# An encoder layer on one core: the down weights' differences loaded and stored through GpSimd's queue, with each store in two halves

## The chip, the cores and the metric

The kernel runs on one core of one Trainium2 chip. The metric is the device time of one execution in microseconds (us). Three executions are known of the kernel before; the median is 1974.39 us.

## The reference, cut to what matters

One encoder layer on 1024 tokens plus 16 meta tokens, width 1024, all in float32. The part that matters here is the last one, a SwiGLU block with 2816 hidden columns:

```python
h2 = rmsnorm(h_res, norm2_w[l])
gu = h2 @ w_gate_up[l]                                    # 1024 x 5632
h_res = h_res + (jax.nn.silu(gu[..., :D_FF]) * gu[..., D_FF:]) @ w_down[l]   # 2816 x 1024
out = rmsnorm(h_res, final_norm_w)
```

## The kernel before, in words

**Precision.** TensorE multiplies operands of the type float32r. Every float32 operand is split in a high part (ScalarE, L101, a CAST) and a low part (VectorE, L102, a subtraction), and a product is three matmuls for each slice of the inner dimension.

**Fewer products.** Matrix products are made in the manner of Strassen: the operands are cut in 2 x 2 blocks, sums and differences of blocks are formed first, and seven block products stand for eight. The down projection at the end of the kernel (L2025 and on) needs such differences of blocks of `w_down`. They depend on weights alone, so the kernel makes them earlier, beside another stage, and parks them in DRAM in the tensors `t_d[0..10]`, from which the end reads them back (L2048 in the profile).

**The gate and up stage.** The loop at L1966 runs over 22 pairs of column blocks (gate and up), j = 0 to 21; the first ones are opened ahead of it in an order written out by hand, which ends at L1965. From there the framework's scheduler sets the order at build time: on each engine the instructions stand in one fixed order and are executed in that order, and an instruction that waits holds all that stand behind it on its engine. A pair is seven products (L1446, twelve matmuls each) into PSUM banks: P1 and P2 (part1, L1764), then S2, S1, S3, S4 and TT (L1986 to L1996). P1, S2, S3 and TT share one bank. Between them the bank has to be read: after P1 and after S2 by ScalarE (L1769, L1987), after S3 by VectorE (`add(u3, b1, u3)`, L1991, recorded as L1412 with `b<-pd,b`). In this document that last one is called **the S3 add**. TT can't start before it has ended; only the product S4 lies between S3 and TT. ScalarE copies the bank of S1 (L1989) ahead of S4 in the same way. VectorE also makes the sums and low parts of the next pair's weights (L1420 to L1423, L102).

**The differences of the down weights.** After pair j, for j = 4 to 14, the loop calls `down_sums(j - 4, ...)` (L2001, function at L1776). One call is a **block**, k = 0 to 10. It takes the tile `r` of 128 x 2 x 1024 (named `sums` in the profile; its pool has one buffer of the tag `al1`, so block k+1 uses the same memory as block k), loads its two halves from `w_down` (L1782, L1783, 512 KB each), makes four subtractions in place on VectorE (recorded as L179 `sums<-sums`), and stores the whole tile to `t_d[k]` (L1786, 1024 KB). The loads and the store are issued by SyncE (SP). Because there is one buffer, the loads of block k+1 wait until the store of block k has landed. From the first subtraction of a block to the first of the next is called a **turn**.

SyncE's queue also holds the loads of the gate and up weights (L1759, L1760, into `raw` tiles) and the stores of the activations (L1998, L1999), in an order that the scheduler made.

Of the kernel before, what the change touches and what calls it, by code (L numbers as in the profile page):

```python
# [16 lines left out]
P = 128  # L17
# [31 lines left out]
def encoder_layer(ctx: ExitStack, tc: tile.TileContext, x, meta, norm1_w, w_in, w_ba,  # L49
                  dn_conv_w, A_log, dt_bias, dn_norm_w, sc_conv_w, w_bdn, w_bsc,  # L50
                  w_out, norm2_w, w_gu, w_down, final_w, out):
    nc = tc.nc
    x, out = x[0], out[0]
    w_out, w_down = w_out[0], w_down[0]
# [10 lines left out]
    def uid(s):  # L65
        cnt["n"] += 1
        return f"{s}_{cnt['n']}"
# [110 lines left out]
    def sub(out, a, b):  # L178
        nc.vector.tensor_tensor(out=out, in0=a, in1=b, op=ALU.subtract)  # L179
# [1570 lines left out]
    HK = NF // 2  # L1750
    t_d = [dr.tile([P, 2, D], F32, name=f"t_d{k}") for k in range(HK)]
# [24 lines left out]
    def down_sums(k, behind):  # L1776

        r = ap_.tile([P, 2, D], F32, tag="al1", name=uid("sums"))
        if k == 0:
            nc.scalar.copy(r[:, 0, 0:1], behind[:, 0:1])  # L1780
        b11, b12, b21, b22 = (r[:, i // 2, 512 * (i % 2):512 * (i % 2) + 512] for i in range(4))
        nc.sync.dma_start(r[:, 0], w_down[k * P:k * P + P, :])  # L1782
        nc.sync.dma_start(r[:, 1], w_down[(HK + k) * P:(HK + k + 1) * P, :])  # L1783
        for o_, a, b in ((b11, b12, b11), (b12, b22, b12), (b22, b22, b11), (b21, b21, b22)):
            sub(o_, a, b)
        nc.sync.dma_start(t_d[k], r)  # L1786


    def load_pair(j, spread=False):
# [176 lines left out]
    for j in range(2, NF):  # L1966
# [12 lines left out]
        if j >= HK:  # L1979
            k = j - HK  # L1980
# [19 lines left out]
        if 4 <= j <= HK + 3:  # L2000
            down_sums(j - 4, sg)  # L2001
# [147 lines left out]
```

## Time and profile before

| | us |
|---|---|
| three executions | 1973.14, 1974.39, 1974.99 |
| the profiled execution, whole | 1973.36 |
| its span, first to last instruction | 1971.6 |
| TensorE (PE) busy in the span | 1957.3 |
| VectorE (DVE) busy | 1398.0 |
| ScalarE (ACT) busy | 837.7 |
| GpSimd (POOL) busy, all of it before 970 us | 108.4 |

The gate and up stage lies from about 970 us to 1760 us of the span; the blocks of `down_sums` are worked on from 1434.6 us to 1577.3 us. A row of the profile names the line, the engine, the operation and the tiles (output, then inputs). In a timeline the first number is the start in the span and the second the duration, both in us; the brackets say how long the engine was idle ahead of it and for what. `SPq` is a transfer's issue on SyncE; PEld is TensorE's weight load.

### The profile page before, as it was taken

To read this page: it belongs to the slowest core of one execution; us is meant where nothing else is said; L and a number is where in the kernel's file an instruction comes from. 1 tells how busy PE (TensorE), PEld (TensorE's weight loads), DVE (VectorE), ACT (ScalarE), POOL (GpSimd) and SP (SyncE) were. 2 spreads that over 40 slices of the span, in tenths; PEclk is the share of its full clock that TensorE was granted. 3 is DMA by queue.
4 is the path that set the end of the run, shared out by engine and by line. 5 is a ranking of instruction groups with operands and counts; after the bars stand their busy time and mean duration, and the time that the engine had idled before them with its cause. 6 is when DMAs were issued, how large, how long until landed. Compare 5 with 4: busy or idle time off the path is not lost.

```text
span 1971.6 us, 31923 instructions
## 1 busy us (share of the span) xinstructions
PE 1957.3 (99%) x11992; PEld 1719.6 (87%) x11992; DVE 1398.0 (71%) x3017; ACT 837.7 (42%) x1968; POOL 108.4 (5%) x410
## 2 busy tenths in 40 slices
PE   9999999999999999999999999999999999999998
PEld 8999999999999999888888888888888888878887
DVE  7888688888888888845954544468676765746575
ACT  6462364646464646343444211235333333324344
POOL 2011101010101010100000000000000000000000
PEclk9999999999999999999999999999999999999999
DMA  4122121212121212223246642133366654577654
GB/s 145 61 86 81 55 87 60 77 59 77 59 84 52 87 49 87 65 81 108 85 150 242 245 153 86 65 107 112 103 234 246 245 189 153 178 274 242 193 173 168
DMA packets 124704, 251.53 MB, mean 128 GB/s; under 512 B 44988, under 2 KB 46453, under 8 KB 122117
## 3 DMA queue, kind: packets, MB, share of 16 engines
q1 hardware_dynamic: 123957, 248.44, 37.8%
q8 instruction: 94, 1.54, 0.3%
q10 hardware_dynamic: 592, 1.05, 0.1%
q14 instruction: 61, 0.50, 0.1%
HBM read 181.20 MB, written 68.25 MB: 127 GB/s over the span
## 4 chain that ended last, share of the span: by engine, by line
PE 45%; DMA 3%; DVE 2%; ACT 1%; issue 0%; SPq 0%; DVEq 0%; ACTq 0%
PE pd L1446 12%; PE pe L1446 6%; PE pm L1446 4%; PE pe L2057 1%; PE pe L2055 1%; PE pe L2056 1%; PE pd L2057 1%; PE pd L2055 1%; PE pd L2056 1%; PE pe L134 1%; PE pe L135 1%; PE pd L135 1%; PE pd L134 1%; PE pe L136 1%; PE pd L136 1%; PE pm L2056 1%
## 5 line engine op out<-in xcount | busy, mean ns | idle before, releaser
L328 PE MATMUL pm<-hTh,wh 128*128 128x320 f32 (+4 forms) x1248 | 426.9, 347 | 0.3 <-ACT hTh L1096 0.2
L328 PE MATMUL pm<-hTh,wl 128*128 128x320 f32 (+4 forms) x1248 | 426.8, 347 | 0.0
L328 PE MATMUL pm<-al,wh 128*128 128x320 f32 (+4 forms) x1248 | 423.8, 345 | 0.0
L328 PEld LDWEIGHTS pm<-hTh,wh 128*128 128x128 f32 x1248 | 233.9, 188 | 10.7 <-ACT hTh L1096 0.9
L328 PEld LDWEIGHTS pm<-al,wh 128*128 128x128 f32 x1248 | 233.8, 188 | 10.7
L328 PEld LDWEIGHTS pm<-hTh,wl 128*128 128x128 f32 x1248 | 233.9, 188 | 10.2 <-POOL wl L1111 0.3
L102 DVE TENSOR_TENSOR al<-raw,ring_h 128x1024 fp32r<-128x1024 f32 x73 | 88.6, 1222 | 65.6 <-ACT ring_h L101 64.7
L101 ACT CAST ring_h<-raw 128x1024 fp32r<-128x1024 f32 x73 | 76.6, 1053 | 109.1 <-PE pe L2057 35.0
L982 DVE TENSOR_TENSOR wl<-raw,wh 128x512 fp32r<-128x512 f32 x112 | 75.3, 687 | 34.5 <-ACT wh L985 34.2
L350 DVE SCALAR_TENSOR_TENSOR kq<-ra,wc,kq 128x520 f32<-128x520 f32 x128 | 96.5, 754 | 3.5 <-ACT kq L380 2.0
L878 ACT ACTIVATE w<-pd,small 128x128 f32<-128x128 f32 x128 | 39.8, 362 | 123.4 <-PE pd L871 122.9
L483 DVE TENSOR_TENSOR tm<-fP,fN 128x135 f32<-128x135 f32 (+23 forms) x248 | 72.2, 291 | 4.8
L487 DVE TENSOR_TENSOR fP<-fP,tm 128x135 f32<-128x135 f32 (+23 forms) x248 | 71.9, 290 | 5.0
L985 ACT CAST wh<-raw 128x512 fp32r<-128x512 f32 x112 | 66.3, 624 | 3.8 <-issue 3.6
L101 ACT CAST wh<-raw 128x1024 fp32r<-128x1024 f32 x37 | 38.8, 1047 | 47.8 <-PE pe L135 10.4
L1994 ACT ACTIVATE b<-b 128x512 f32<-128x512 f32 x20 | 12.6, 632 | 101.6 <-DVE b L1412 101.6
L843 ACT ACTIVATE jk<-NP 128x128 f32<-128x128 f32 x64 | 19.9, 311 | 81.1 <-DVE NP L839 80.1
L102 DVE TENSOR_TENSOR wl<-raw,wh 128x1024 fp32r<-128x1024 f32 x37 | 45.1, 1219 | 10.2 <-ACT wh L101 10.0
L1446 PE MATMUL pd<-b_hl,wh 128*128 128x512 f32 x168 | 51.9, 390 | 0.0
L1412 DVE TENSOR_TENSOR b<-pd,b 128x512 f32<-128x512 f32 x21 | 14.5, 689 | 52.5 <-PE pd L1446 47.5
L350 DVE SCALAR_TENSOR_TENSOR vT<-ra,wc,vT 128x520 f32<-128x520 f32 x64 | 48.3, 754 | 1.4 <-ACT vT L380 0.7
L679 POOL TENSOR_TENSOR tm<-mP,mN 1x15 f32<-1x15 f32 (+7 forms) x120 | 36.9, 307 | 210.8 <-DMA mN<-ndm 202.4
(630 smaller groups left out, 4772.1 us busy)
## 6 DMA issues: line engine op xcount, KB each, us to landing
raw<-in_w_in_dram SPq DMA_DIRECT2D x72, 512.0 KB
raw<-in_w_gate_up_dram SPq DMA_DIRECT2D x44, 512.0 KB
sums<-in_w_down_dram SPq DMA_DIRECT2D x22, 512.0 KB
t_d<-sums SPq DMA_DIRECT2D x11, 1024.0 KB
raw<-s_d SPq DMA_DIRECT2D x44, 256.0 KB
raw<-t_d SPq DMA_DIRECT2D x44, 256.0 KB
act_d<-b SPq DMA_DIRECT2D x43, 256.0 KB
raw<-act_d SPq DMA_DIRECT2D x33, 256.0 KB
```

The costliest lines, as they stand in the source:

```text
L101: nc.scalar.copy(hi, src)
L102: nc.vector.tensor_tensor(out=lo, in0=src, in1=hi.bitcast(F32), op=ALU.subtract)
L134: mm(po[:m, :n], wh[:, k, :m], xhk[:, t0:t0 + n], start=(k == 0), stop=False)
L328: mm(po[:, :n], ww[:, k], f(k)[:, t0:t0 + n], start=i == 0, stop=i == 3 * KT - 1)
L350: nc.vector.scalar_tensor_tensor(out=acc, in0=raw[:, h0 + t:h0 + t + hn], scalar=wc[:, t, col:col + 1], in1=acc, op0=ALU.mult, op1=ALU.add)
L483: nc.vector.tensor_tensor(out=tv, in0=fP[:, 0:r, j:j + 1].broadcast_to([P, r, n]), in1=fN[:, j:j + 1, j + 1:32].broadcast_to([P, r, n]), o ...
L487: nc.vector.tensor_tensor(out=fP[:, 0:r, j + 1:32], in0=fP[:, 0:r, j + 1:32], in1=tv, op=ALU.subtract)
L878: nc.scalar.activation(w[d], b2[:, 2 + d], AF.Copy, scale=ce[:, c, d:d + 1])
L982: nc.vector.tensor_tensor(out=u[1][1][:, k], in0=u[2][:, k], in1=u[1][0][:, k].bitcast(F32), op=ALU.subtract)
L985: nc.scalar.copy(u[1][0][:, k], u[2][:, k])
L1446: mm(po, x[:, k], at(y, k), start=i == 0 and not add_to, stop=i == 11, skip_group_check=add_to)
L2056: mm(bank[t], h_[:, c], l_[:, hi], start=False, stop=False)
```

## The change

The two loads and the store of `down_sums` are issued by GpSimd in place of SyncE, and the store is cut in two: the first half of the tile is stored after the second subtraction, the other after the fourth. The arithmetic is the same.

```diff
-        nc.sync.dma_start(r[:, 0], w_down[k * P:k * P + P, :])
-        nc.sync.dma_start(r[:, 1], w_down[(HK + k) * P:(HK + k + 1) * P, :])
-        for o_, a, b in ((b11, b12, b11), (b12, b22, b12), (b22, b22, b11), (b21, b21, b22)):
+        nc.gpsimd.dma_start(r[:, 0], w_down[k * P:k * P + P, :])
+        nc.gpsimd.dma_start(r[:, 1], w_down[(HK + k) * P:(HK + k + 1) * P, :])
+        for i, (o_, a, b) in enumerate(((b11, b12, b11), (b12, b22, b12), (b22, b22, b11), (b21, b21, b22))):
             sub(o_, a, b)
-        nc.sync.dma_start(t_d[k], r)
+            if i % 2:
+                nc.gpsimd.dma_start(t_d[k][:, i // 2], r[:, i // 2])
```

From L1787 on, a line of the kernel after has a number that is one higher. TensorE's order is the same in both kernels. The orders of SyncE, GpSimd, VectorE and ScalarE differ.

**SyncE and GpSimd, around block 1.** On SyncE before, the transfers of blocks 0 and 1 stand among the gate and up loads and the activation stores:

```order
L1760 DMA raw_15892<-in_w_gate_up_dram 128x1024
L1759 DMA raw_15891<-in_w_gate_up_dram 128x1024
L1786 DMA t_d_14752<-sums_15505 128x2048
L1782 DMA sums_15631<-in_w_down_dram 128x1024
L1783 DMA sums_15631<-in_w_down_dram 128x1024
L1999 DMA act_d_14735<-b_2350_14860 128x512
L1998 DMA act_d_14735<-b_2350_14860 128x512
L1786 DMA t_d_14753<-sums_15631 128x2048
```

After, they stand on GpSimd's queue alone, behind its last MEMSET; in the brackets are the semaphores for which each waits (DMASW is one of GpSimd's transfers, DVE VectorE):

```order
L1783 DMA sums_15505<-in_w_down_dram 128x1024 [waits DVE_49,PE_49]
L1782 DMA sums_15505<-in_w_down_dram 128x1024 [waits Activation_49]
L1787 DMA t_d_14752<-sums_15505 128x1024 [waits DMASW1_49,DVE_49]
L1787 DMA t_d_14752<-sums_15505 128x1024 [waits DMASW0_49,DVE_49]
L1782 DMA sums_15632<-in_w_down_dram 128x1024 [waits DMASW3_49,DMASW2_49]
L1783 DMA sums_15632<-in_w_down_dram 128x1024
```

33 transfers leave SyncE's queue and 44 come to GpSimd's. The first load of a block waits for both half stores of the block ahead (DMASW2 and DMASW3).

**VectorE in pair 6.** `pd_15647` before and `pd_15649` after are the same bank, pair 6's; `sums_15756` and `sums_15758` are block 2. Before:

```order
L102 TENSOR_TENSOR wl_15890<-raw_15891,wh_15889 128x1024
L102 TENSOR_TENSOR s_hl_15092<-raw_15766,s_hl_15092 128x1024
L179 TENSOR_TENSOR sums_15756<-sums_15756 128x512
L1412 TENSOR_TENSOR b_2350_14860<-pd_15647,b_2350_14860 128x512
L179 TENSOR_TENSOR sums_15756<-sums_15756 128x512 x3
L1412 TENSOR_TENSOR b_2350_14860<-pe_15686,b_2350_14860 128x512
```

After:

```order
L102 TENSOR_TENSOR s_hl_15092<-raw_15769,s_hl_15092 128x1024
L102 TENSOR_TENSOR wl_15894<-raw_15895,wh_15893 128x1024
L179 TENSOR_TENSOR sums_15758<-sums_15758 128x512 x3
L1412 TENSOR_TENSOR b_2350_14860<-pd_15649,b_2350_14860 128x512
L179 TENSOR_TENSOR sums_15758<-sums_15758 128x512
L1412 TENSOR_TENSOR b_2350_14860<-pe_15688,b_2350_14860 128x512
```

Ahead of the S3 add (`<-pd`) stood one subtraction of block 2, and three stand there now.

**VectorE in pair 11.** `pd_16272` before and `pd_16279` after are pair 11's bank; `sums_16659` is block 9 before, and `sums_16806` is block 10 after. Before:

```order
L102 TENSOR_TENSOR mB_14825<-raw_16403,mB_14825 128x1024
L102 TENSOR_TENSOR wl_16539<-raw_16540,wh_16538 128x1024
L179 TENSOR_TENSOR sums_16659<-sums_16659 128x512 x3
L1412 TENSOR_TENSOR b_2350_14860<-pd_16272,b_2350_14860 128x512
L179 TENSOR_TENSOR sums_16659<-sums_16659 128x512
```

After:

```order
L102 TENSOR_TENSOR wl_16548<-raw_16549,wh_16547 128x1024
L102 TENSOR_TENSOR mB_14825<-raw_16411,mB_14825 128x1024
L179 TENSOR_TENSOR sums_16806<-sums_16806 128x512 x2
L1412 TENSOR_TENSOR b_2350_14860<-pd_16279,b_2350_14860 128x512
L179 TENSOR_TENSOR sums_16806<-sums_16806 128x512 x2
```

Before, the S3 add of pair 11 stands behind three subtractions of block 9, and block 10 is not begun until pair 12; now it stands behind two subtractions of block 10, the last one.

## The prediction

> **What bounds the kernel now.** I read the page's busy row first, then the stretch in which the blocks run, then who waits there, and last the chain of waits. The page's first part:
>
> ```profile
> span 1971.6 us, 31923 instructions
> PE 1957.3 (99%) x11992; PEld 1719.6 (87%) x11992; DVE 1398.0 (71%) x3017; ACT 837.7 (42%) x1968; POOL 108.4 (5%) x410
> ```
>
> TensorE is idle for 14.3 us in all, so no change that leaves its products alone can gain more than that. The stretch from 1430 to 1580 us holds all subtractions of the blocks; the view by stretches gives the length, then each engine's busy time and count, the granted clock, the DMA share and the rate:
>
> ```profile
> 1430.00:1580.00 150.00, 149.89 (x662) 123.80 (x661) 108.39 (x150) 51.29 (x72) 0.00 (x0) 1.00 0.67 242
> ```
>
> TensorE is busy in 149.89 of 150 us, at the full granted clock (1.00), and GpSimd is empty. Of the waits in that stretch, here is the only one of TensorE, and then four of the others (total, times, longest):
>
> ```profile
> PEld pd L1446 <- DVE b L1412: 0.5, 1, 0.5
> ...
> DVE sums L179 <- DMA sums<-in_w_down_dram: 16.1, 7, 4.2
> ...
> SPq L1786 <- DVE sums L179: 27.2, 11, 3.8
> SPq L1786 <- DMA sums<-in_w_down_dram: 18.2, 7, 5.1
> SPq L1782 <- DMA t_d<-sums: 15.2, 8, 4.2
> ```
>
> VectorE stands for 16.1 us in front of subtractions whose loads haven't landed; SyncE stands in front of this function's store and loads for more. Yet TensorE lost 0.5 us. So the waits are there, and they are covered. How thin the cover is shows in the chain of waits (start, duration, what):
>
> ```profile
> 1521.63 2.73 PE pd L1446 x12
> 1532.32 4.42 DMA t_d<-sums
> 1536.76 5.10 DMA sums<-in_w_down_dram
> 1541.98 0.69 DVE sums L179
> ...
> 1551.87 5.78 DMA sums<-in_w_down_dram
> 1557.74 0.70 DVE sums L179
> 1559.08 0.69 DVE b L1412
> 1559.82 5.74 PE pd L1446 x24
> ```
>
> For 35 us the chain leaves TensorE and runs through a store, loads and subtractions to the S3 add of pair 11. The blocks' turns are already the tightest thing beside TensorE.
>
> **What is removed.** 33 issues on SyncE, and with them the 27.2 + 18.2 us in which it stands in front of L1786 and the 15.2 us in front of L1782, so the gate and up loads behind them can go earlier. I cost this at nothing: in the stretch no row of the waits has ScalarE or VectorE waiting for a `raw` load, so nobody is late for those. At best the 0.5 us of TensorE goes.
>
> **What is moved: one turn more.** The deadline is read at pair 11 in the timeline (start, duration):
>
> ```profile
> 1554.11 2.88 PE L1446 MATMUL pd<-b,s_hl 128*128 128x512 f32 x12
> 1556.83 2.88 PE L1446 MATMUL pe<-b,s_hl 128*128 128x512 f32 x12
> 1559.82 2.56 PE L1446 MATMUL pd<-b,u_hl 128*128 128x512 f32 x10
> ...
> 1434.62 0.68 DVE L179 TENSOR_TENSOR sums<-sums 128x512 f32<-128x512 f32 x1
> ...
> 1556.01 0.69 DVE L179 TENSOR_TENSOR sums<-sums 128x512 f32<-128x512 f32 x1 [2.16 <-DMA sums<-in_w_down_dram]
> 1557.74 1.42 DVE L179 TENSOR_TENSOR sums<-sums 128x512 f32<-128x512 f32 x2 [1.04 <-DMA sums<-in_w_down_dram]
> 1559.08 0.68 DVE L1412 TENSOR_TENSOR b<-pd,b 128x512 f32<-128x512 f32 x1
> ```
>
> S3 and S4 start 2.72 us apart, so TT was due at 1556.83 + 2.72 = 1559.55; it began at 1559.82, 0.27 late, behind the S3 add. Block 0's first subtraction began at 1434.62 and block 9's at 1556.01: nine turns of (1556.01 - 1434.62) / 9 = 13.49 us, and with these the kernel before is just in time. In the new order block 10, not 9, stands ahead of this add, with two subtractions. A run of two and the add took from 1557.74 to 1559.08, so to be in time block 10 has to start by 1557.74 - 0.27 = 1557.47. That is **ten turns in 122.85 us, 12.29 us each**. With turns of 13.49 it would be 134.9 - 122.85 = 12.05 us late. VectorE keeps to its order, so the S3 add waits for it, then TT, then every product behind. In pair 6, with three subtractions ahead of the S3 add in place of one, the same wait comes early, so the lateness is paid in pieces along pairs 6 to 11.
>
> **What the new transfers do to a turn.** A turn in the old kernel, with the sizes of the transfers, from the timeline and the issues:
>
> ```profile
> 1453.16 0.32 SPq L1786 DMA_DIRECT2D t_d<-sums  x1
> ...
> 1457.04 0.33 SPq L1782 DMA_DIRECT2D sums<-in_w_down_dram  x1
> 1457.42 0.42 SPq L1783 DMA_DIRECT2D sums<-in_w_down_dram  x1
> ...
> 1461.73 0.69 DVE L179 TENSOR_TENSOR sums<-sums 128x512 f32<-128x512 f32 x1 [3.31 <-DMA sums<-in_w_down_dram]
> ...
> sums<-in_w_down_dram SPq DMA_DIRECT2D x22, 512.0 KB
> t_d<-sums SPq DMA_DIRECT2D x11, 1024.0 KB
> ```
>
> The store takes 3.9 us until the first load may go, and 4.7 us later the first subtraction starts.
>
> Half a store: the first half goes while subtractions three and four run, so the second half alone, 512 KB, is left on the path. I take off what 0.524 MB cost at the rate of the busiest stretch that I looked at:
>
> ```profile
> 1458.00:1463.00 5.00, 5.00 (x24) 4.13 (x23) 1.69 (x3) 0.59 (x1) 0.00 (x0) 1.00 0.94 346
> ```
>
> At 346 GB/s that is 1.5 us less per turn. GpSimd's issues: three lie in a row on a turn's path (second half store, first load, second load, which the second subtraction needs). The trace has no transfer issued by GpSimd. The nearest rows are issues of the same transfers on SyncE (least, median, most, in ns):
>
> ```profile
> L1783 SPq DMA_DIRECT2D sums<-in_w_down_dram x11: 328/432/1093, 1365.4 to 1569.5; - x11
> L1786 SPq DMA_DIRECT2D t_d<-sums x11: 319/326/327, 1440.0 to 1577.4; - x11
> L2048 SPq DMA_DIRECT2D raw<-t_d x44: 429/432/1475, 1791.8 to 1934.8; - x44
> ```
>
> From 0.33 to 1.475 us; I take the middle, 0.90, in place of 0.33, 0.33 and 0.43: 0.57 + 0.57 + 0.47 = 1.6 us more per turn. What comes after the issue I take as on SyncE. So a turn is 13.49 - 1.5 + 1.6 = 13.6 us, and ten are 136.
>
> GpSimd has nothing else to do (0.00 busy in the stretch), so issues there delay nobody but the blocks. That a third queue is used at all costs something only outside the stretch, for which the whole profiled run has 1973.36 - 1971.6 = 1.8 us; I take nothing.
>
> **Two rules of the skill.** The Trainium skill, "DMA: Bandwidth & Descriptors", section "Issuing engines are not separate DMA queues", says that all issuers share the same 16 engines and that another issuer saves only its issue time. The trace agrees as far as it goes: an issue is 0.33 us on SyncE. The same page, "Latency and other measured facts", puts the first byte at about 0.6 us for SyncE's way and 1 us for GpSimd's. No run here shows either; with 0.4 us more on a store and on a load, the turn would be 12.8 us and the sum 5 us.
>
> **The sum.** 136 - 122.85 = 13.1 us late, less the 0.5 us that TensorE lost already: +12.6 us on the profiled execution's own 1973.36, **1986.0 us**. The median of the runs before, 1974.39, lies 1.0 above that execution.
>
> Bounds. With issues at 0.33 us the turn is 12.0, under 12.29: nothing late, 1973.36 - 0.5 = 1972.9. With issues at 1.475 (+1.15, +1.15, +1.04) and loads like the chain's slow ones (5.78 for 4.7) the turn is 13.49 - 1.5 + 3.3 + 1.1 = 16.4, so 164 - 122.85 - 0.5 = +41, 2014.
>
> **The rivals.**
>
> *In time after all, not slower.* If a turn through GpSimd takes at most 12.29 us, block 10 is ready, TensorE stays full, and the time is 1972.9. What decides is 1.2 us per turn against 13.49, and the halved store alone could give it. For it: few subtractions waited for a load (count, busy time and mean, idle time ahead of them),
>
> ```profile
> L179 DVE TENSOR_TENSOR sums<-sums 128x512 f32<-128x512 f32 x44 | 30.2, 687 | 16.5 <-DMA sums<-in_w_down_dram 16.1
> ```
>
> 7 of 44 by the row above, so part of 13.49 may be the old order's own pace. Against it: SyncE's issue of 0.33 us would have to hold for GpSimd.
>
> *Far slower: GpSimd held up by VectorE.* VectorE is busy 108.39 of 150 us. If each issue had to let the running VectorE instruction end, at most the longest here,
>
> ```profile
> L102 DVE TENSOR_TENSOR mB<-raw,mB 128x1024 fp32r<-128x1024 f32 x8 | 9.7, 1220 | 0.2
> ```
>
> then three of 1.22 us per turn make it 13.6 + 3.7 = 17.3 and the sum 173 - 123.35 = +50, 2023. Against it: nothing in the stretch shows the two engines meeting. The Trainium skill, "SBUF — State Buffer", section "SBUF: two separate sides", has this as its "DVE blocks DMA" trap, but only beside VectorE's two-port modes, which a two-input operation like these rows doesn't use; by that rule it would not come.
>
> *SyncE relieved, a real gain.* The whole cover is 0.5 us, so this can't reach 0.2%.
>
> **How the numbers follow.** Forecast (5 to 25 us slower) 0.5; in time after all 0.22; 25 to 41 us slower 0.18; held up by VectorE 0.08; a gain by something not seen 0.02. The time given is the forecast's, 1986; the range 1972.9 to 2014 takes in the bounds of the issue cost and leaves out the held-up case. About 0.2% (3.9 us) is what a measurement of this kernel can tell from no change. Slower by more: 0.5 + 0.18 + 0.08 = 0.76; within: 0.21; faster: 0.03.
>
> **What would show it.** Right: TensorE's busy time is unchanged, its idle time in pairs 6 to 11 is some 13 us, ended by the S3 add (L1412) or by ScalarE's copy (L1988) that stands behind it; VectorE's wait for `sums` grows from 16.1 us; block 10's first subtraction starts near 1570, not by 1557.5; the old queue's row falls by some 23 MB and another queue has them. The issue cost is read as the gap between GpSimd's two loads of a block. Wrong: TensorE full with the blocks done early (issue cheap), gaps of whole VectorE instructions ahead of GpSimd's issues, or idle time elsewhere, at the end above all, where `t_d` is read.

## The result, and the profile after

| | us |
|---|---|
| before, median of six | 1974.22 (1973.04 to 1976.26) |
| after, median of six | 1987.62 (1985.41 to 1992.16) |
| ratio, 95% interval | 1.0074 (1.0063 to 1.0085) |
| the profiled execution of after, whole | 1990.61 |

The kernel is 13.4 us slower by the medians; 1986.0 was forecast. The page of after, its busy row and its two large queues (packets, MB, share):

```profile
span 1988.9 us, 31974 instructions
...
PE 1963.4 (99%) x11992; PEld 1723.7 (87%) x11992; DVE 1399.6 (70%) x3017; ACT 837.9 (42%) x1968; POOL 131.2 (7%) x454
...
q1 hardware_dynamic: 119205, 225.37, 34.2%
q0 software_dynamic: 6336, 23.07, 3.2%
```

The span grew by 1988.9 - 1971.6 = 17.3 us. TensorE does the same 11992 matmuls, yet its busy time is not the same: 1963.4 in place of 1957.3, 6.1 us more. Its idle time went from 14.3 to 25.5 us. So the profiled execution paid 11.2 us in standing still and 6.1 us in slower matmuls. About 2 us of the idle time is not the change's: the wait of TensorE in front of L98, far ahead of the blocks, was 0.9 us in before and 2.8 in after, and lies anywhere from 0.7 to 2.4 us in the kernels below.

Where it was paid is shown by stretches of one old pair each (length; busy time and count of PE, PEld, DVE, ACT, POOL; granted clock; DMA share; rate):

```profile
1467.10:1486.10 19.00, 18.79 (x83) 15.56 (x84) 13.30 (x19) 6.49 (x9) 2.67 (x5) 1.00 0.70 248
1486.10:1505.20 19.10, 15.91 (x67) 12.87 (x66) 12.05 (x17) 6.38 (x9) 3.19 (x6) 0.95 0.54 193
1505.20:1524.20 19.00, 19.00 (x81) 15.23 (x80) 9.69 (x16) 2.94 (x5) 2.67 (x5) 0.96 0.57 204
1524.20:1543.20 19.00, 15.08 (x55) 12.13 (x55) 12.99 (x19) 5.79 (x9) 2.68 (x5) 0.82 0.62 233
1543.20:1562.30 19.10, 19.10 (x86) 15.82 (x85) 10.32 (x15) 6.07 (x9) 3.19 (x6) 1.00 0.65 233
1562.30:1581.30 19.00, 17.10 (x68) 13.65 (x67) 14.85 (x22) 5.50 (x8) 3.21 (x6) 0.91 0.66 242
```

A full stretch holds 86 matmuls, as in the fifth row. The fourth holds 55: TensorE stood 3.9 us without a matmul, and the granted clock was 0.82 as the mean of the stretch (0.50 for 6.83 us, from 1527.14 us on). The waits of after between 1429 and 1600 us, TensorE's two and VectorE's longest:

```profile
PE pd L1446 <- ACT b L1988: 9.0, 3, 3.9
PE pd L1446 <- DVE b L1412: 0.8, 1, 0.8
...
DVE sums L179 <- DMA sums<-in_w_down_dram: 31.1, 15, 5.7
```

VectorE's wait for the loads of the blocks went from 16.1 us (7 times) to 31.1 us (15 times). TensorE seldom waits for the S3 add itself; it waits for ScalarE's copy after S2 (L1988). How one becomes the other shows in the timeline of the longest stall, three engines together (start, duration, in brackets the idle time ahead and its end):

```profile
1519.77 0.69 DVE L179 TENSOR_TENSOR sums<-sums 128x512 f32<-128x512 f32 x1 [5.02 <-DMA sums<-in_w_down_dram]
...
1522.33 0.68 DVE L1421 TENSOR_TENSOR raw<-raw,raw 128x512 f32<-128x512 f32 x1
...
1523.10 1.05 ACT L101 CAST mB<-raw 128x1024 fp32r<-128x1024 f32 x1 [6.28 <-DVE raw L1421]
...
1527.59 0.58 ACT L1988 COPY b<-pd 128x512 f32<-128x512 f32 x1
...
1521.42 2.88 PE L1446 MATMUL pm<-s,s_hl 128*128 128x512 f32 x12
1528.22 5.49 PE L1446 MATMUL pd<-b,s_hl 128*128 128x512 f32 x12 [3.92 <-ACT b L1988]
```

VectorE stood 5.02 us in front of block 6's first subtraction. Behind it stood the sums of weights (L1420 to L1423), which have nothing to do with the block; behind these ScalarE's casts (6.28 us idle ahead of the first); behind the casts the copy that frees the bank of S2; behind the copy TensorE. And when TensorE went on, its twelve matmuls took 5.49 us, where the product before took 2.88.

One turn through GpSimd, from the second half store of block 0 to block 1:

```profile
1442.26 0.53 POOL L1787 DMA_DIRECT2D t_d<-sums  x1 [2.94 <-DVE sums L179]
1445.72 0.54 POOL L1782 DMA_DIRECT2D sums<-in_w_down_dram  x1 [2.93 <-DMA t_d<-sums]
1446.24 0.53 POOL L1783 DMA_DIRECT2D sums<-in_w_down_dram  x1
...
1449.84 0.69 DVE L179 TENSOR_TENSOR sums<-sums 128x512 f32<-128x512 f32 x1 [0.27 <-DMA sums<-in_w_down_dram]
...
1574.63 0.69 DVE L179 TENSOR_TENSOR sums<-sums 128x512 f32<-128x512 f32 x1 [2.72 <-DMA sums<-in_w_down_dram]
```

The issue takes 0.53 us (the gap between the two loads is 0.52), the store holds the load back for 3.46 us, and 4.12 us later the subtraction starts. Block 10 begins at 1574.63 and block 0 began at 1436.60: ten turns of 13.80 us. The ten turns of before have the same mean (1434.62 to 1572.66), as its order leaves block 10 to pair 12; its first nine took 13.49 us each, and the first nine of after 13.88.

### The profile page after: what moved, and what is told of

Same layout as the page of the kernel before. It is cut to its first block, busy times and chain, and to the rows that moved or that the text cites. A ratio compares the mean times of both kernels' runs of the same rounds, so it can differ in the third digit from the quotient of the medians.

```text
span 1988.9 us, 31974 instructions
## 1 busy us (share of the span) xinstructions
PE 1963.4 (99%) x11992; PEld 1723.7 (87%) x11992; DVE 1399.6 (70%) x3017; ACT 837.9 (42%) x1968; POOL 131.2 (7%) x454
## 4 chain that ended last, share of the span: by engine, by line
PE 41%; DMA 5%; DVE 3%; issue 1%; ACT 1%; POOL 0%; SPq 0%; DVEq 0%; POOLq 0%; ACTq 0%
PE pd L1446 10%; PE pe L1446 5%; PE pm L1446 3%; DMA sums<-in_w_down_dram 2%; DMA t_d<-sums 2%; PE pe L2058 1%; PE pe L2056 1%; PE pe L2057 1%; PE pd L2058 1%; PE pd L2056 1%; PE pd L2057 1%; PE pe L136 1%; PE pe L135 1%; PE pd L136 1%; PE pd L135 1%
## 5 line engine op out<-in xcount | busy, mean ns | idle before, releaser
L101 ACT CAST wh<-raw 128x1024 fp32r<-128x1024 f32 x37 | 38.8, 1048 | 46.1 <-PE pe L135 10.4
L1995 ACT ACTIVATE b<-b 128x512 f32<-128x512 f32 x20 | 12.6, 632 | 106.6 <-DVE b L1412 106.6
L843 ACT ACTIVATE jk<-NP 128x128 f32<-128x128 f32 x64 | 19.9, 311 | 81.1 <-DVE NP L839 80.1
L102 DVE TENSOR_TENSOR wl<-raw,wh 128x1024 fp32r<-128x1024 f32 x37 | 45.1, 1219 | 10.4 <-ACT wh L101 10.3
L179 DVE TENSOR_TENSOR sums<-sums 128x512 f32<-128x512 f32 x44 | 30.3, 690 | 31.4 <-DMA sums<-in_w_down_dram 31.1
```

The source lines that it names most:

```text
L101: nc.scalar.copy(hi, src)
L102: nc.vector.tensor_tensor(out=lo, in0=src, in1=hi.bitcast(F32), op=ALU.subtract)
```

## The experiments

The theory, and what stands against it, by the letters that the expectations use. **T**: VectorE executes in the order fixed at build time; that order puts the subtractions of a block where a turn of some 12.3 to 12.8 us would have their data ready; a turn through GpSimd is longer, and each lateness goes down the line of engines shown above. **Q**: GpSimd's queue has a price by itself, wherever the blocks stand. **H**: it is the halving of the store, which makes the scheduler set the blocks earlier, whatever the queue. **C** is about the lower clock alone. Each median is of 5 to 11 executions, and each ratio is to executions of the kernel before taken beside them, whose median was 1972.90 us for the three kernels with stores, loads or chosen starts, and 1974.04 to 1974.26 for the others. The ladder, in the section on the lower clock, was executed once. "Asked" is worked out as in the prediction: the start that a block needs to be ahead of a pair's S3 add, divided by the turns up to it.

| kernel | median, us | ratio to before, 95% interval |
|---|---|---|
| halves on SyncE | 1975.90 | 1.0007 (0.9999 to 1.0016) |
| whole stores on GpSimd | 1984.65 | 1.0056 (1.0044 to 1.0068) |
| half stores on GpSimd, loads on SyncE | 1977.96 | 1.0025 (1.0015 to 1.0035) |
| loads on GpSimd, half stores on SyncE | 1982.39 | 1.0050 (1.0037 to 1.0062) |
| one block per pair, GpSimd, halves | 1980.07 | 1.0027 (1.0014 to 1.0040) |
| one block per pair, SyncE, whole | 1977.48 | 1.0016 (1.0008 to 1.0025) |
| loads in four, GpSimd, halves | 1981.25 | 1.0039 (1.0024 to 1.0055) |
| loads in four, SyncE, halves | 1974.37 | 1.0002 (0.9994 to 1.0011) |
| chosen starts, GpSimd, halves | 1991.75 | 1.0093 (1.0080 to 1.0106) |
| a MEMSET ahead of the loads, GpSimd | 1988.11 | 1.0067 (1.0054 to 1.0080) |

### The two halves of the change apart

Only the halving, all transfers on SyncE:

```diff
-        for o_, a, b in ((b11, b12, b11), (b12, b22, b12), (b22, b22, b11), (b21, b21, b22)):
+        for i, (o_, a, b) in enumerate(((b11, b12, b11), (b12, b22, b12), (b22, b22, b11), (b21, b21, b22))):
             sub(o_, a, b)
-        nc.sync.dma_start(t_d[k], r)
+            if i % 2:
+                nc.sync.dma_start(t_d[k][:, i // 2], r[:, i // 2])
```

> The kernel before with each store in two halves: the halving alone. VectorE's order is then close to that of the changed kernel (six whole blocks ahead of pair 8's S3 add, nine ahead of pair 10's, ten ahead of pair 11's, where there ten and two subtractions stand). In time this needs turns of 12.8 us up to pair 10. Theory T: a turn on SyncE with half a store left on its path is 13.49 less 0.5 to 1.5 us, 12.0 to 13.0, so 0 to 2 us are lost: 1973 to 1977 us. Rival H (the order with more turns ahead of the deadlines costs the same whatever the queue): 1985 to 1989 us.

1975.90 us, as T had it. The order here is nearly that of the changed kernel (VectorE has finished three blocks, not two and three subtractions, ahead of pair 6's S3 add, and ten, not ten and two, ahead of pair 11's; the same between). H by itself is out: the order with the blocks set earlier costs 0.07% on SyncE, and the interval takes in no difference. In the traced execution, the slowest of the eleven, VectorE waited 19.9 us for the blocks' loads, against 31.1 in after.

Only the queue, the store whole (the edit is to the changed kernel):

```diff
-            if i % 2:
-                nc.gpsimd.dma_start(t_d[k][:, i // 2], r[:, i // 2])
+        nc.gpsimd.dma_start(t_d[k], r)
```

> The changed kernel with each store whole: the queue alone is changed. VectorE's order is then close to that of before (ahead of pair 11's S3 add stands one subtraction of block 9, before it was three, and no block 10), so ten turns in 122.85 us are not asked, but nine in 123.5, 13.72 each. Theory T: the whole store takes its old time and GpSimd adds 0.26 us of wake-up and 0.2 us of issue at a store and again at the loads, a turn of about 14.2 us, 9 x 0.5 = 4.5 us late and 1 to 3 us for TensorE's lower clock behind a stall: 1978 to 1983 us. Rival H (it is the halving alone that does it, through the order with a turn more): 1973 to 1975 us.

1984.65 us, above T's 1978 to 1983 and far from H. A turn in this kernel (store, load, subtraction):

```profile
1452.45 0.54 POOL L1786 DMA_DIRECT2D t_d<-sums  x1 [7.67 <-DVE sums L179]
1456.93 0.53 POOL L1782 DMA_DIRECT2D sums<-in_w_down_dram  x1 [3.94 <-DMA t_d<-sums]
...
1463.94 0.69 DVE L179 TENSOR_TENSOR sums<-sums 128x512 f32<-128x512 f32 x1 [6.50 <-DMA sums<-in_w_down_dram]
```

Its waits between 1429 and 1600 us, VectorE's longest and TensorE's two:

```profile
DVE sums L179 <- DMA sums<-in_w_down_dram: 31.9, 12, 6.5
...
PE pd L1446 <- ACT b L1987: 5.3, 4, 2.7
PE pd L1446 <- DVE b L1412: 4.1, 3, 1.8
```

The queue alone costs 10.4 us with an order close to that of before, which asks for 13.72 us per turn ahead of pair 11. The ten turns took 15.2 us each, where 14.2 had been expected: some loads were slow, like this one with 7.01 us from issue to subtraction. So the lateness is there without the tenth turn. This falls on the prediction too, and is taken up below.

The pieces of a turn, from the timelines (the least of ten or eleven, then the median, us; in the last row the mean of the first nine turns):

| | SyncE whole | SyncE half | GpSimd whole | GpSimd half |
|---|---|---|---|---|
| last subtraction's end to store issue | 0.03, 0.03 | 0.03, 0.03 | 0.29, 0.30 | 0.29, 0.30 |
| store issue to load issue | 3.87, 4.07 | 2.67, 4.29 | 4.42, 4.70 | 3.44, 3.55 |
| load issue to first subtraction | 4.00, 4.84 | 3.64, 3.83 | 4.02, 4.83 | 3.85, 4.18 |
| the three together, mean | 9.0 | 8.0 | 10.1 | 8.9 |

By the least values half a store in place of a whole one saves 1.2 us on SyncE and 1.0 on GpSimd, and GpSimd costs 0.26 + 0.77 + 0.21 = 1.24 us per turn with halves and 0.26 + 0.55 + 0.02 = 0.83 with whole stores. The means of the whole path agree: the half saves 1.0 and 1.3 us, and GpSimd costs 0.9 us with halves and 1.2 with whole stores. The medians of single pieces don't (with halves the store's piece is longer on SyncE, 4.29 to 3.55), as a piece also holds time in which an engine stood elsewhere in its order. Note the two outer columns: the path of the changed kernel, 8.9 us, is no longer than that of before, 9.0. It is late because its order asks for more.

### Stores and loads apart

```diff
  (stores alone on GpSimd, against before; the loop as above)
-        nc.sync.dma_start(t_d[k], r)
+            if i % 2:
+                nc.gpsimd.dma_start(t_d[k][:, i // 2], r[:, i // 2])
  (loads alone on GpSimd, against the changed kernel)
-                nc.gpsimd.dma_start(t_d[k][:, i // 2], r[:, i // 2])
+                nc.sync.dma_start(t_d[k][:, i // 2], r[:, i // 2])
```

> Half stores on GpSimd's queue, loads back on SyncE's. VectorE's order has the same number of subtractions ahead of every S3 add as with half stores on SyncE alone (12.8 us per turn asked up to pairs 8 and 10). Theory T, with the pieces measured so far: turns on SyncE with half stores 11.0 to 12.3 us where no order held them, GpSimd's later store issue (0.3 in place of 0.0 us after the last subtraction) and 0.2 to 0.4 us more until it has landed make 12 to 12.5: in time, 1974 to 1978 us. Rival Q (a store through GpSimd is what costs, whatever the order asks): 1983 to 1989 us.

> Loads on GpSimd's queue, half stores back on SyncE's. VectorE's order asks more than that of the changed kernel: three subtractions of block 7 ahead of pair 9's S3 add and three of block 10 ahead of pair 11's, 11.9 and 12.2 us per turn. Theory T: turns of 11.7 (SyncE, halves) + 0.2 to 0.5 for GpSimd's slower issue and wake-up at the loads = 12 to 12.3, short by 0.1 to 0.4 in each of seven to ten turns: 1 to 4 us, with 1 to 2 us of lower clock, 1975 to 1980 us. Rival Q (loads through GpSimd cost by themselves): 1983 to 1989 us. Rival H (only the order counts): above the changed kernel, over 1988 us.

The stores alone: 1977.96 us, at the upper end of T. The number of subtractions ahead of every S3 add is here the same as with halves on SyncE, so this is the queue alone at an equal order, and the turn is longer by the 0.26 us of the store issue, and 0.33 us at the least until the load may go (3.00 for 2.67). It costs 0.25% where SyncE's halves cost 0.07%. The loads alone: 1982.39 us, over T's 1975 to 1980 and under what Q or H gave; this order asks 11.9 us per turn ahead of pair 9, and the turns' median was 13.07. But the before beside these two was 1972.90 us, some 1.3 lower than the expectations had it, so 5.1 and 9.5 us were lost: a little more than T allowed for the stores, and for the loads about where Q's range begins. The two together cost about what the change does (0.25% and 0.50%, and 0.74%).

### Room for a turn

Each block held back to its own pair, first on GpSimd, then on SyncE:

```diff
-        if k == 0:
-            nc.scalar.copy(r[:, 0, 0:1], behind[:, 0:1])
+        nc.scalar.copy(r[:, 0, 0:1], behind[:, 0:1])
```

> The changed kernel, with one line's condition taken away: every block, not only block 0, is held back by ScalarE's small copy until its own pair's activation is there, so that one block is made per pair, with 19.04 us from one to the next where a turn needs 13 to 14. Theory T (the turn is too long for the place that the fixed VectorE order gives each block): nobody waits for a block any more, TensorE's idle time and clock return to those of before, 1973 to 1975 us. Rival Q (loads and stores on GpSimd's queue cost something by themselves, wherever the blocks stand): 1985 to 1989 us still, as the same 44 transfers go through that queue.

> The kernel before (SyncE's queue, whole stores), with every block held back in the same way until its own pair. Theory T: TensorE was short of 0.5 us at most in the stretch of the blocks, so 1973 to 1974.5 us, no difference that can be measured from before. Rival Q: the same here, and the difference between this kernel and its twin on GpSimd's queue is then the queue's own price, 12 us or so; by theory T it is under 2 us.

1980.07 and 1977.48 us: neither T's 1973 to 1975 nor Q's 1985 to 1989, and 2.6 us between the twins, where T had under 2 and Q 12. The stretches of the GpSimd kernel tell why: pairs 5 to 11, pairs 12 to 16, and five pairs without blocks:

```profile
1429.00:1562.28 133.28, 133.28 (x589) 110.40 (x588) 89.44 (x121) 47.64 (x70) 14.99 (x28) 1.00 0.56 194
1562.28:1657.48 95.20, 88.87 (x374) 71.94 (x373) 67.37 (x96) 31.33 (x45) 8.03 (x15) 0.96 0.71 237
1657.48:1752.68 95.20, 95.20 (x422) 78.83 (x421) 60.39 (x82) 32.85 (x45) 0.00 (x0) 1.00 0.51 174
```

In pairs 5 to 11, where the changed kernel lost most (7.9 of its 9.8 us of standing), TensorE is busy for 133.28 of 133.28 us at full clock, with the same transfers on the same queue in halves. For these pairs Q is out. What is lost is lost in pairs 13 to 15, where the last blocks now stand beside the loads and stores of the next stage's sums (L1983 and L2010 in the kernel before), with the DMA share at 0.71 in place of 0.56 and the median of the blocks' loads, from issue to landing, at 6.0 us in place of 4.0. So holding the blocks back seems to have brought them where they don't fit (that these transfers are the cause was not tried by itself): a side effect that T's expectation had left out, and one that SyncE pays too (2.9 us there, 2.4 of it in one stall).

Each load cut in two by partitions, nothing held back, on either queue (half stores):

```diff
-        nc.gpsimd.dma_start(r[:, 0], w_down[k * P:k * P + P, :])
-        nc.gpsimd.dma_start(r[:, 1], w_down[(HK + k) * P:(HK + k + 1) * P, :])
+        for i in range(2):
+            for p in (slice(0, 64), slice(64, 128)):
+                nc.gpsimd.dma_start(r[p, i], w_down[(HK * i + k) * P + p.start:(HK * i + k) * P + p.stop, :])
```

> The changed kernel with each of the two loads cut in two by partitions: the same bytes on the same GpSimd queue, 66 transfers in place of 44, nothing held back. The scheduler now counts on a longer turn and sets the subtractions further back by itself: five whole blocks stand ahead of pair 8's S3 add (six in the changed kernel), seven ahead of pair 10's (nine), eight and one subtraction ahead of pair 11's (ten and two). That asks turns of 15.4 us or more, and the two more issues of 0.53 us make a turn of 13.1 + 1.1 = 14.2 us. Theory T (the price is where VectorE's fixed order puts the subtractions against when their data really come): nobody is late, TensorE is full in pairs 5 to 12, 1973 to 1976 us, though the queue does more than in the changed kernel. Rival Q (GpSimd's queue costs by itself): more transfers, 1988 us or above.

> The same cut of the loads with all transfers on SyncE's queue and half stores. The order asks still less (nine whole blocks ahead of pair 12's S3 add). Theory T: 1973 to 1975 us, no difference from before that can be measured, and within 2 us of the same kernel on GpSimd's queue. Rival Q: 12 us or so below its twin on GpSimd's queue.

On SyncE 1974.37 us, no difference from before. On GpSimd 1981.25 us: 6 us under the changed kernel with 22 transfers more on the queue, but 5 above T's range, and 6.9 above its twin, where T had 2. Its stretches:

```profile
1429.00:1562.28 133.28, 132.07 (x582) 108.70 (x581) 89.74 (x122) 44.35 (x63) 26.18 (x50) 1.00 0.69 211
1562.28:1657.48 95.20, 90.62 (x392) 74.21 (x391) 68.04 (x95) 31.46 (x44) 7.38 (x14) 0.98 0.67 219
```

The same picture: 1.2 us in pairs 5 to 11, where after lost 133.28 - 125.36 = 7.9 at a clock of 0.96, and the rest in the pairs behind. There one store took until 8.9 us after its issue before the load could go, against 3.5 us mostly.

Blocks held to chosen steps of chosen pairs by a copy on GpSimd (the key names the pair and the step behind which the block is called: `s` after part1, `u2` and `u3` after ScalarE's copies of S2 and S1, `a3` after the S3 add, `a2` after the add of S4, `sg` at the pair's end):

```diff
-        if k == 0:
-            nc.scalar.copy(r[:, 0, 0:1], behind[:, 0:1])
+        nc.gpsimd.tensor_copy(r[:, 0, 0:1], behind[:, 0:1])
...
+    PACE = {(4, 'sg'): 0, (5, 'a2'): 1, (6, 'u3'): 2, (7, 'u2'): 3, (7, 'sg'): 4, (8, 'a2'): 5, (9, 'u3'): 6,
+            (10, 's'): 7, (10, 'sg'): 8, (11, 'a3'): 9, (12, 'u2'): 10}
```

> The changed kernel with each block held back, by a one-column copy on GpSimd into its buffer, until a chosen step of a chosen pair (13 to 16 us apart), so that the scheduler itself sets the blocks further back: five whole blocks stand ahead of pair 8's S3 add, where six stood, and nine ahead of pair 11's, where ten and two subtractions stood. That asks 15 to 16 us per turn, and a turn through GpSimd takes 13 to 14. Theory T: TensorE isn't held up in pairs 5 to 11; 1973 to 1976 us, the queue and the halves being the same as in the changed kernel. Rival Q: 1985 to 1989 us.

1991.75 us, the slowest of all, and the expectation fell. Block 3 in pair 7 (GpSimd, VectorE, TensorE):

```profile
1476.92 0.18 POOL L1779 COPY sums<-b 128x1 f32<-128x1 f32 x1 [4.00 <-ACT b L1994]
1477.40 0.54 POOL L1781 DMA_DIRECT2D sums<-in_w_down_dram  x1 [0.30 <-POOL sums L1779]
...
1483.35 1.42 DVE L179 TENSOR_TENSOR sums<-sums 128x512 f32<-128x512 f32 x2 [6.50 <-DMA sums<-in_w_down_dram]
1484.68 0.68 DVE L1412 TENSOR_TENSOR b<-pd,b 128x512 f32<-128x512 f32 x1
...
1485.42 2.79 PE L1446 MATMUL pd<-b,u_hl 128*128 128x512 f32 x11 [2.76 <-DVE b L1412]
```

The load may go at 1477.40, after ScalarE's copy of S2's bank, and its data are used 5.95 us later; yet the order puts two subtractions of that block ahead of the same pair's S3 add. The turns were long enough; what was asked in vain was the way from a load's issue to its data. So T has to be put more widely: not the length of the turn counts, but that the fixed order supposes each transfer's data sooner than they come. This wider form was made after the run, and no run here was made to try it. This run does not speak against Q by its time, only by the row that names the cause.

A small MEMSET on GpSimd ahead of the loads:

```diff
+        nc.gpsimd.memset(r[:, 0, 0:1], 0.0)
         nc.gpsimd.dma_start(r[:, 0], w_down[k * P:k * P + P, :])
```

> The changed kernel with one small MEMSET of a column on GpSimd ahead of the loads of every block. The scheduler then sets ten whole blocks ahead of pair 11's S3 add, in place of ten and two subtractions, eight ahead of pair 10's in place of nine, and five in place of six ahead of pair 8's: 13.5 us per turn asked in place of 12.3. A turn is that of the changed kernel with 0.1 to 0.4 us for the MEMSET, 13.2 to 14.2. Theory T: from in time to 9 x 0.7 = 6 us late, with 1 to 3 us of lower clock, 1974 to 1983 us, in any case under the changed kernel. Rival Q: 1986 to 1990 us.

1988.11 us, Q's number. But the turn was not 13.2 to 14.2 us; it was 15.1:

```profile
1441.69 0.10 POOL L1782 MEMSET sums<- 128x1 f32 x1 [2.47 <-DMA t_d<-sums]
1442.18 0.54 POOL L1784 DMA_DIRECT2D sums<-in_w_down_dram  x1 [0.38 <-issue]
1442.70 0.53 POOL L1783 DMA_DIRECT2D sums<-in_w_down_dram  x1
```

The scheduler turned the two loads round: the half that the first subtraction needs (L1783) now goes second, and from the first issue to the first subtraction it was 6.6 us in the median where the changed kernel had 4.18. By its time the run tells T and Q not apart; its premise, a turn like that of after with a less pressing order, did not come about.

Counted over all ten kernels of the table, and by the times as they stand, T's range held for three: halves on SyncE, the stores alone on GpSimd, and loads in four on SyncE. All six with the loads on GpSimd's queue came out above it, and so did the held-back kernel on SyncE. Shown is that neither the earlier blocks by themselves (0.07% with halves on SyncE) nor the queue by itself (TensorE full in pairs 5 to 11 with the blocks held back) cost what the change costs; how much the loads through GpSimd cost, T put too low each time.

### The lower clock

```diff
+        for _ in range({15: 8, 17: 11, 19: 14, 21: 18}.get(j, 0)):
+            nc.vector.tensor_tensor(out=u3, in0=u3, in1=u3, op=ALU.max)
         add(u3, b1, u3)
```

> The kernel before with 8, 11, 14 and 18 more VectorE operations (the maximum of u3 with itself) ahead of the S3 add in pairs 15, 17, 19 and 21, which has no blocks beside it. A row of two such takes 0.605 us more per operation, so TT should begin about 1.0, 2.8, 4.6 and 7.1 us late, 15.5 us in all. Theory C (behind a stall of over some 2 us TensorE runs at half the granted clock for a while, which is part of the change's price): TensorE's busy time grows by 1.5 to 2.5 us behind each of the three longer stalls and not behind the short one, and the span by 20 to 23 us. Rival (the lower clock in the changed kernel had another cause): granted clock 1.00 behind every stall and a span 15 to 16 us longer.

Neither: the one execution took 1970.74 us (span 1969.0), and there were no stalls to look behind. 51 more operations made VectorE's busy time 34 us longer (1432.4 for 1398.0), and TensorE waited 0.2 us for all of it. The order shows why. In pair 15, here against that of before (+ is what the new one has there), the scheduler had put the next pair's first matmuls in front of TT (`u_hl`), which has to wait for the longer chain:

```
 L1446 MATMUL pm_16863<-b_2372_14935,s_hl_15092 128x512 x12
+L1446 MATMUL pd_16957<-b_hl,wh_16949 128x512 x2
+L1446 MATMUL pd_16957<-b_hl,wl_16950 128x512
...
 L1446 MATMUL pd_16820<-b_2371_14934,u_hl_15044 128x512 x12
```

For C it gives nothing, but it is a good contrast for T: work that the scheduler sees at build time it covers, 34 us of it on VectorE; lateness that it doesn't see costs TensorE a few us per stall.

For C there are the stalls that the other runs made anyway. In the thirteen profiled executions (before, after and the eleven kernels above) TensorE's timeline has 57 gaps of over 0.5 us between 970 and 1785 us. Behind none of the 37 shorter than 1.8 us did more than the first matmul run slowly; behind 15 of the 20 from 1.90 to 4.37 us, at once or up to five matmuls later, 7 to 13 matmuls came at half the rate, which cost 1.6 to 1.7 us each time (once 2.8); behind five (1.90 to 3.18 us) they did not. The granted clock says the same: 0.50 for 3.41 us behind each of the 15 (6.83 us behind the longest of after), and nowhere else in that time. In after three gaps did, 3.2, 3.9 and 1.9 us long: 1.56 + 2.76 + 1.70 = 6.0 us, the 6.1 us by which TensorE's busy time grew. C holds by these counts, though not by the experiment made for it.

## Why the prediction was right, and where it was not

**Nothing to gain.** Right: no kernel here was faster than before by more than its measurement can tell, and the best, with loads in four on SyncE, is at 1.0002.

**One turn more.** The size came out right, in part by luck (below): ten turns of 13.6 us, 136, were forecast, and ten of 13.80, 138.0, came. Block 0 began 2.0 us later (the wait far ahead of the blocks, above), so block 10 had to start by 1557.47 + 2.0 = 1559.5 and started at 1574.6, 15.1 us late. TensorE lost 9.8 us of standing (170 us from 1430 to 1600 with 160.17 busy, 0.1 idle before) and 6.0 of clock there, 15.8 together. But where the step makes the added turn the cause, it failed. Without it, with whole stores on GpSimd, 10.4 us are lost; with nearly the same order on SyncE, 1.6. What the runs show in its place: the halving shortens a turn by 1.0 to 1.3 us, and the order that comes with it asks for the blocks that much earlier; the queue lengthens a turn by 0.8 to 1.2 us, for which neither order leaves room. On SyncE both orders are in time or nearly so, on GpSimd neither is. The prediction's own terms would have given both: 13.49 + 1.6 = 15.1 us for whole stores on GpSimd, where 13.72 are asked, and 13.49 - 1.5 = 12.0 for halves on SyncE, where 12.8 are asked.

**Half a store, -1.5 us.** Measured -1.0 on SyncE and -1.3 on GpSimd by the means of the whole path: the rate of a busy stretch put the saving somewhat too high.

**Three issues on GpSimd, +1.6 us.** Measured +1.24 by the least pieces and +0.9 by the means, made up otherwise. The issue was put at 0.90 us and is 0.53 (531 to 548 ns for the 22 stores, 532 to 542 for the loads but one of 780); but the way from one step to the next, taken as on SyncE, is longer: 0.26 us from the subtraction to the store's issue, and more until the load's issue, which starts 0.56 us after the store has landed (once 0.83). The Trainium skill, "DMA: Bandwidth & Descriptors", "Latency and other measured facts", puts GpSimd's way 0.4 us later at the first byte; on the store, 0.77 us were added, of which the longer issue explains 0.2, so the rule points the right way, and on the load, with 0.21, it is hardly seen. What of the added time is a later first byte and what a later start of the next issue these runs do not part, as the traces have no landings of SyncE's transfers. The two errors cancel in part. With the half store, +0.1 us per turn was forecast, and the path came out 0.1 us shorter (8.9 for 9.0). What made the first nine turns 0.4 us longer lies between a block's first and last subtraction (5.0 us for 4.5), which the sum had left as it was; so the 13.6 met the 13.80 by other terms than its own.

**What ends TensorE's wait.** The S3 add was named first and ScalarE's copy second; it is the copy, 9.0 of 9.8 us, by way of the next pair's sums and casts that stand behind the block on VectorE. The sum does not change by that, since all hang on VectorE's order.

**TensorE's busy time unchanged.** Wrong: +6.1 us. The forecast had no term for the clock. That the sum came out near is luck to that extent: in the profiled execution the standing time alone, 9.8 us in the stretch, would have been less than the +12.6 forecast, and the two errors in part make up for each other.

**The rivals.** In time after all: no, but the halving alone would have been (1975.90 us). GpSimd held up by VectorE: a store's issue starts 0.29 to 0.57 us after the subtraction and a load's 0.56 to 0.83 us after the store has landed, less than the 1.22 us of the longest VectorE instruction; the second load follows the first by 0.52 us (once 0.73) while VectorE works. SyncE relieved: nothing seen. Nor did GpSimd's transfers make SyncE's late: between 1429 and 1640 us no row of the waits, in before, in after or in any kernel on GpSimd's queue, has an engine waiting for a gate or up load (`raw`). The end of the kernel, where `t_d` is read: TensorE is busy in 150.00 of 150 us in both, from 1790 us before and from 1807.3 after.

**Left open.** What makes single stores and loads slow (6.4 us for a median of 2.9, 7.6 for 4.7), and so how much of the 13.80 us is GpSimd's and how much the meeting with SyncE's transfers, stays open; so does why every kernel with its loads on GpSimd lost more than T had for it. The order of the changed kernel was not run word for word on SyncE.

## What to carry to other kernels

Where a scheduler fixes each engine's order at build time, a change of queue, or of the number of transfers, is also a change of that order: lay out for each block when its data are asked for and when the trace says they can be there, along every engine that stands behind. A wait on an engine with time to spare is not free when work for the bottleneck stands behind it in the same order, as the weights' sums stood behind the subtractions here. And count a stall of TensorE of some two microseconds or more as perhaps 1.7 us longer than it is (15 of 20 here).

## What the runs showed of the hardware that was not expected

- The lower clock begins behind shorter gaps than one would guess from the Trainium skill, "TensorE: Matmul & The Clock Gate", section "Part 1: The HAM clock gate", which has the clock fall to half after an idle window of about 3.4 us whose start is independent of the program. Half rate and nothing between agrees with these traces (twelve matmuls in 5.49 us for 2.88), and so does that the gap's length alone doesn't decide (one of 3.18 us left the clock as it was, one of 1.90 lowered it); but gaps of 1.90 to 2.75 us were enough ten times here, and that measurement decides.
- An issue of 512 KB took GpSimd 0.53 us (once 0.78), where SyncE mostly takes 0.33 to 0.43; and a store's started 0.29 us after the subtraction that released it (three times of 22, 0.57), where SyncE's started 0.03 us after.
